# A hybrid SSD and attention layer on one Trainium2 core: ScalarE's own silu, modulation products in other places, and output weights split later

## The chip, the core and the metric

The kernel runs on one core of a Trainium2 chip. The core has a matrix engine (TensorE, PE in the profile; PEld is its weight load) and three engines for elementwise work: VectorE (DVE), ScalarE (ACT) and GpSimd (POOL). SyncE (SP) issues DMA transfers. Each engine takes its instructions in a fixed order, and waits on semaphores for the others. Matmuls write PSUM, and VectorE and ScalarE carry results from there into SBUF. The metric is the time of one execution on the device in microseconds (us), lower is better; the median of three runs is given.

## The reference, cut to what matters

One layer over 1024 tokens with D = 1024: a mixer with an SSD branch and an attention branch, then a convolutional feed-forward network (FFN). The vector c makes shifts, scales and gates (the modulations).

```python
mod = (silu(c) @ w_ada + b_ada)                       # 6 x 1024
sh_m, sc_m, g_m, sh_f, sc_f, g_f = split(mod, 6)
h = rmsnorm(x, norm_mix_w) * (1 + sc_m) + sh_m
z, xbc, dt_raw, q, k, v = split(h @ w_in, IN_SPLITS)  # 512, 1024, 8, 512, 512, 512
xbc = silu(causal_dwconv(xbc, conv_w) + conv_b)       # width 4; split into xs, B, C
dt = softplus(dt_raw + dt_bias);  A = -exp(a_log)
y = ssd_scan(xs * dt, dt * A, B, C) + d_skip * xs
y_ssd = rmsnorm(y * silu(z), ssd_norm_w)
y_att = chunk_attention(q, k, v, rel_bias)            # own chunk and 8 before it
x = x + g_m * (concat[y_ssd, y_att] @ w_out)
h = rmsnorm(x, norm_ffn_w) * (1 + sc_f) + sh_f
g, val = split(causal_dwconv(h @ w_up, ffn_conv_w), 2)
x = x + g_f * ((silu(g) * val) @ w_down)
return rmsnorm(x, final_norm_w)
```

All is float32.

## The kernel before

Each float32 matmul is made of three in a rounded format: both operands are split into a high part (a rounded copy, on ScalarE) and a low part (source minus high, on VectorE or GpSimd), and high x high, high x low and low x high are added in PSUM (`mm3`, L75 to L78; `split`, L80 to L86). The helper `split` with a scale does the rounding as a scaled copy (L82) and the low part as one VectorE operation (L83).

The span of 1223 us runs through these stages.

- To about 97 us: the modulations that the first norm needs, h transposed, and q, k, v. A modulation column is one VectorE product with a running sum, 128x1024, over 512 KB of w_ada that a DMA brings (`mod_col`, L134).
- To 319.5 us: attention, chunk by chunk. Its scheduling leaves VectorE places for modulation products; the last number of `MODS` says how many the end of attention takes.
- To about 375 us: the eight 128-channel tiles of xbc, `conv_silu`: B and C of each group (bt, ct), then the four of xs (xst). Per tile there are 48 matmuls into two banks (`s`), a scaled copy by ScalarE, three shifted VectorE products with a sum (L519), and silu as tanh (L524, ScalarE) and a product (L525, VectorE); the weights were halved ahead for that. Behind each tile's last such product `conv_mods` issues the number of modulation products that `CMODS` names, through three SBUF areas called wos. The weights of six of these tiles get their low part on GpSimd (L86, wl). The xs tiles are transposed by TensorE (tp, L597).
- To 424.9 us: z and dt_raw, as two halves of 260 columns (`z_tile`), half 1 first, eight row tiles of 24 matmuls each per half. A tile leaves PSUM by a tanh (L655, zt) and a VectorE product (L656, zs). Meanwhile the output weights w_out come in by DMA in eight slots (`wout_get`), go through three wos areas and two raws areas (`stage`), four of them are multiplied by the gate (`wout_fold`) and all are split (`wout_split`: slots 0 to 3 as 128x1024, slots 4 to 7 in two halves with the SSD norm's weight as a scale). `dt_prep` works out dt and the decays.
- To 531 us: the SSD in eight chunks. For each, `ssd_pre` makes the decay matrices of two groups (rm, sg, then an exponential L738 and a product L739), one chunk ahead; `ssd_y` does the state and output matmuls (ydp, yop, stp), adds, multiplies by silu(z) (L835) and normalises (L837 on ScalarE, two small GpSimd operations L116 and L117, L839 on ScalarE); `ssd_turn` transposes. Between them stand halves of the output projection (`wout_half`, tiles wops): half n takes the attention part (n even) or the SSD part (n odd) of a row tile. Each right side for it is split one half ahead (`wout_rhs`, yhl).
- To about 600 us: the second norm, h transposed, and the sums of a Strassen scheme for the FFN; the first products P1 of two units (uX) overlap with it. The rest is the FFN's units, to about 1000 us, and the down projection.

The order on each engine is fixed when the program is built: a scheduler takes the instructions in about the order in which the code is written, by their dependences and priorities, and `issue_after` or a pin forces one instruction behind another. `wout_split` is issued behind the last `ssd_pre` by two such pins (`pin`). Buffers are pools with a number of rotating tiles; a tile is free once its last reader is done. From `T.on = True`, and later `V.on = A.on = True`, TensorE, VectorE and ScalarE take the code's own order (`InOrder`; those rows have the line L58).

The loop over the chunks reads:

```python
for c in range(NT):
    y = ssd_y(c, *pre)
    if turn: ssd_turn(*turn)
    turn = (c, y)
    if c < NT - 1:
        pre = ssd_pre(c + 1, x_tile, sg_tile, lambda: wout_half(c, slice(0, 3)))
        row_scale(pin[0])
        wout_half(c, slice(3, 8))
```

Of the kernel before, what the change touches and what calls it, by code (L numbers as in the profile page):

```python
# [27 lines left out]
MODS = (0, 1, 1, 12)  # L28
CMODS = (1, 2, 2, 2, 2, 3, 3, 3)
# [35 lines left out]
def tile_block(ctx: ExitStack, tc: tile.TileContext, x, crep, pk, w_ada, w_first, w_ft, w_z,  # L65
# [145 lines left out]
    V.tensor_scalar(pkt[:, SCW:FCW], pkt[:, SCW:FCW], 0.5, None, op0=ALU.mult)  # L211
# [300 lines left out]
    def conv_silu(ft, dst, th2):  # L512
        wh, wl = early.pop(ft) if ft in early else wu_pair(w_ft[ft], A, G)
        ps = s_tile()
        gemm_ft(wh, wl, [ps[:, 0:512], ps[:, 512:1024]])
        w = [pkt[:, SCW + 4 * ft + j:SCW + 4 * ft + j + 1] for j in range(4)]
        A.activation(dst, ps, AF.Identity, scale=w[3], bias=pkt[:, SCB + ft:SCB + ft + 1])
        for j in range(1, 4):
            V.scalar_tensor_tensor(dst[:, j:S], ps[:, 0:S - j], w[3 - j], dst[:, j:S],  # L519
                                   op0=ALU.mult, op1=ALU.add)  # L520
        for hh in range(2):
            c = slice(hh * 512, hh * 512 + 512)
            th = th2()
            A.activation(th, dst[:, c], AF.Tanh)  # L524
            last = V.scalar_tensor_tensor(dst[:, c], th, 1.0, dst[:, c], op0=ALU.add, op1=ALU.mult)  # L525
        return last.ins
# [37 lines left out]
    na = bcp.tile([P, 16], F32, name="na")[:, 0:8]  # L564
# [15 lines left out]
    for g in range(2):  # L580
        conv_mods(2 * g, conv_silu(4 + g, bt_[g], th512))
        conv_mods(2 * g + 1, conv_silu(6 + g, ct_[g], th512))
# [8 lines left out]
    for ft in range(4):  # L591
        xt = bcp.tile([P, S], F32, tag="rm", bufs=2, name="xst")
        conv_mods(4 + ft, conv_silu(ft, xt, th512))
        for hh in range(2):
            tps = tp_tile()
            for j in range(4):
                T.transpose(tps[:, j * P:(j + 1) * P], xt[:, (4 * hh + j) * P:(4 * hh + j + 1) * P],  # L597
                            ident)
            A.activation(xs[:, 4 * hh:4 * hh + 4, ft * P:(ft + 1) * P],
                         tps.rearrange("p (a b) -> p a b", a=4), AF.Copy)  # L600
# [4 lines left out]
    def wout_load(dh, j):  # L605
        t = stage()
# [26 lines left out]
    def wz_weights(ch):  # L633
        ws = []
        for a in range(4):
# [4 lines left out]
            split(th_, tl_, t.rearrange("p (a b) -> p a b", a=2), A, V, scale=0.5)  # L640
            ws.append((th_, tl_))
        return ws

    def z_tile(ch, st, wz):
# [4 lines left out]
        for kt in range(KT):  # L649
# [3 lines left out]
        nz = 260  # L653
        th = wzp.tile([P, 272], F32, tag="zt", bufs=1, name="zt")
        A.activation(th[:, 0:nz], ps[:, 0:nz], AF.Tanh)  # L655
        V.scalar_tensor_tensor(zs[:, st, ch * 260:ch * 260 + nz], th[:, 0:nz], 1.0, ps[:, 0:nz],  # L656
                               op0=ALU.add, op1=ALU.mult)
        if ch == 1:
            V.scalar_tensor_tensor(zs[:, st, 512:520], ps[:, 252:260], 2.0,
                                   pkt[:, DTB:DTB + 8], op0=ALU.mult, op1=ALU.add)  # L660

    def dt_prep():
# [4 lines left out]
        A.activation(na, pkt[:, ALOG:ALOG + 8], AF.Exp)  # L667
# [83 lines left out]
    def wout_get(*slots):  # L751
        for j in slots:
            wt[j] = wout_load(*WORDER[j])
# [51 lines left out]
    def ssd_y(c, xdt, xdd, cb, ms_):  # L805
# [29 lines left out]
        V.tensor_tensor(y, y, zs[:, c, 0:512], ALU.mult)  # L835
# [4 lines left out]
        return y  # L840
# [27 lines left out]
    def wout_rhs(st, part):  # L868
        if st < NT:
            y = yq[st, part] = wu.tile([P, 2, 4, P], F32R, tag="wh", name="yhl")  # L870
            split(y[:, 0], y[:, 1], x1[part][:, st, :].rearrange("p (a b) -> p a b", a=4), A, V)

    def wout_half(n, ks=slice(0, 8), fill=()):
        st, part = n // 2, n % 2
        if ks.start == 0:
# [7 lines left out]
            for q in ((0,), (1, 2))[n] if n < 2 else (n + 1,):  # L883
                wout_rhs(q // 2, q % 2)
# [654 lines left out]
```

## Time and profile before

| what | value |
|---|---|
| median of 3 runs | 1224.7 us (1224.22 to 1227.89) |
| profiled execution: its own time | 1224.97 us |
| its span in the trace | 1223.3 us, 15651 instructions |
| mean granted TensorE clock | 0.99 |
| HBM read, written | 116.56 MB, 29.10 MB |

The busy share of TensorE in 40 slices of 30.6 us each, and the granted clock, in tenths:

| row | slices |
|---|---|
| PE | 5998899989999879999999999999999999999995 |
| PEclk | 9999999999999979999999999999999999999998 |

A digit 9 is 90% or more. The slices with a lower digit lie in the first 100 us, in attention, and around slice 14 (about 398 to 459 us), where the clock has its one 7. A row "PE x <- DVE y: 6.5, 1, 6.5" says that TensorE stood idle for 6.5 us in total, once, ahead of the instruction that writes x, until VectorE's y was done. A row with a time, as in "437.39 0.62 ACT L837 ACTIVATE yt<-yy", has the start in the span, the duration, the engine, the code line, the operation and output<-input.

### The profile page before, as it was taken

What the parts mean: (1) busy time and instruction counts of PE and PEld (TensorE: products, weight loads), DVE (VectorE), ACT (ScalarE), POOL (GpSimd) and SP (SyncE); (2) the same over time, 40 slices, a digit from 0 to 9 for tenths busy, and PEclk for the clock granted to TensorE, in tenths of its full rate; (3) what the DMA queues carried; (4) which work ended last, traced back from release to release, by engine and by line L of the source; (5) the groups of instructions that cost most, each with busy time, mean ns of one, the idle gap of its engine ahead of it and who ended that gap; (6) DMA issues with size and microseconds to landing.
All of it is one profiled execution on the core that took longest, in us unless ns stands there. A gap on an engine that the chain in (4) does not pass through costs nothing.

```text
span 1223.3 us, 15651 instructions
## 1 busy us (share of the span) xinstructions
PE 1161.6 (95%) x5802; PEld 975.8 (80%) x5802; DVE 943.2 (77%) x1421; ACT 588.3 (48%) x991; POOL 195.5 (16%) x172
## 2 busy tenths in 40 slices
PE   5998899989999879999999999999999999999995
PEld 3877787778779868888778888888888888888884
DVE  7846454698698758747999888988889869766976
ACT  4636454663343646666654433444434445433443
POOL 1205563773120124300000000000000000000002
PEclk9999999999999979999999999999999999999998
DMA  9722211314444301132123233232232277733533
GB/s 340 249 56 68 65 50 46 122 67 151 158 168 175 104 1 52 44 121 95 69 78 123 89 116 129 82 108 95 103 129 90 89 283 278 273 115 123 171 120 137
DMA packets 56395, 150.86 MB, mean 123 GB/s; under 512 B 5632, under 2 KB 5760, under 8 KB 54912
## 3 DMA queue, kind: packets, MB, share of 16 engines
q1 hardware_dynamic: 49264, 125.49, 30.3%
q10 hardware_dynamic: 7056, 24.38, 5.0%
q8 instruction: 45, 0.74, 0.3%
q14 instruction: 30, 0.25, 0.1%
HBM read 116.56 MB, written 29.10 MB: 119 GB/s over the span
## 4 chain that ended last, share of the span: by engine, by line
PE 81%; DVE 10%; ACT 3%; DMA 2%; issue 2%; POOL 1%; SPq 0%; DVEq 0%; POOLq 0%; ACTq 0%
PE wops L698 6%; PE dn L76 6%; PE dn L77 6%; PE dn L78 6%; PE uY L78 5%; PE uY L76 5%; PE uY L77 5%; PE uZ L76 3%; PE uZ L77 3%; PE uZ L78 3%; PE uX L76 3%; PE uX L78 3%; PE uX L77 3%; PE acc L76 2%; PE s L76 2%
## 5 line engine op out<-in xcount | busy, mean ns | idle before, releaser
L930 POOL TENSOR_TENSOR st<-st,mhalf 128x1 f32<-128x1 f32 x16 | 12.7, 798 | 689.4 <-DVE st L929 677.7
L76 PE MATMUL dn<-w 128*128 128x512 f32 x308 | 111.9, 389 | 0.0
L77 PE MATMUL dn<-w 128*128 128x512 f32 x308 | 111.9, 389 | 0.0
L418 POOL TENSOR_SCALAR p<-p,st 128x640 f32<-128x640 f32 (+4 forms) x64 | 99.5, 1570 | 42.7 <-DVE st L417 35.7
L78 PE MATMUL dn<-w 128*128 128x512 f32 x308 | 103.3, 389 | 0.0
L76 PE MATMUL uY<-tH,w 128*128 128x512 f32 x248 | 96.5, 389 | 0.0
L77 PE MATMUL uY<-tL,w 128*128 128x512 f32 x248 | 96.5, 389 | 0.0
L78 PE MATMUL uY<-tH,w 128*128 128x512 f32 x248 | 96.5, 389 | 0.0
L85 ACT ACTIVATE w<-ya 128x1024 fp32r<-128x1024 f32 (+1 forms) x41 | 39.1, 955 | 86.0 <-PE uY L78 79.4
L698 PE MATMUL wops<-hH,yhl 128*128 128x512 f32 x224 | 74.8, 402 | 3.5 <-DVE yhl L86 2.1
L77 PEld LDWEIGHTS dn<-w 128*128 128x128 f32 x308 | 57.8, 188 | 12.1
L78 PEld LDWEIGHTS dn<-w 128*128 128x128 f32 x308 | 57.8, 188 | 12.0
L76 PEld LDWEIGHTS dn<-w 128*128 128x128 f32 x308 | 57.8, 188 | 11.9
L85 ACT ACTIVATE w<-xs 128x1024 fp32r<-128x1024 f32 (+1 forms) x41 | 39.1, 954 | 35.6 <-PE uY L78 35.0
L76 PEld LDWEIGHTS uY<-tH,w 128*128 128x128 f32 x248 | 46.5, 188 | 9.7
L78 PEld LDWEIGHTS uY<-tH,w 128*128 128x128 f32 x248 | 46.5, 188 | 9.7
L77 PEld LDWEIGHTS uY<-tL,w 128*128 128x128 f32 x248 | 46.6, 188 | 9.6
L412 DVE CUSTOM_DVE_ANT_0 p<-s,bias 128x640 f32<-128x640 f32 (+4 forms) x64 | 40.4, 651 | 16.8 <-PE tp L444 5.2
L698 PEld LDWEIGHTS wops<-hH,yhl 128*128 128x128 f32 x224 | 42.3, 190 | 12.9 <-DVE yhl L86 2.5
L76 PE MATMUL s<-hH,wh 128*128 128x512 f32 x128 | 50.5, 394 | 1.4 <-DVE ct L519 1.2
L1089 DVE SCALAR_TENSOR_TENSOR a<-cv,pkt,a 128x1023 f32<-128x1023 f32 (+1 forms) x40 | 51.0, 1277 | 0.1
L415 ACT ACTIVATE p<-p,st 128x640 f32<-128x640 f32 (+4 forms) x64 | 44.1, 692 | 13.6 <-DVE st L412 13.3
(449 smaller groups left out, 3414.7 us busy)
## 6 DMA issues: line engine op xcount, KB each, us to landing
gz<-a ACTq DMA_DIRECT2D x10, 1024.0 KB, 5.3
wos<-in_w_ada_dram SPq DMA_DIRECT2D x18, 512.0 KB, 4.1
ya<-in_w_up_dram SPq DMA_DIRECT2D x11, 768.0 KB, 4.0
xs<-in_w_up_dram SPq DMA_DIRECT2D x11, 768.0 KB, 4.1
adat<-in_w_ada_dram SPq DMA_DIRECT2D x16, 512.0 KB, 5.1
raws<-in_w_ft_dram SPq DMA_DIRECT2D x14, 512.0 KB, 4.1
qk<-in_w_ada_dram SPq DMA_DIRECT2D x14, 512.0 KB, 4.6
gy<-a ACTq DMA_DIRECT2D x10, 512.0 KB, 2.6
```

What stands on the lines that cost most here:

```text
L76: T.matmul(ps, lh, rh, start=start, stop=False, skip_group_check=more)
L77: T.matmul(ps, lh, rl, start=False, stop=False, skip_group_check=more)
L78: T.matmul(ps, ll, rh, start=False, stop=stop, skip_group_check=more)
L85: i = A.activation(hi, src, AF.Copy) if ehi is A else ehi.tensor_copy(hi, src)
L412: V.tensor_tensor_reduce(out=dst, in0=src, in1=bsl, scale=-1.0, scalar=3e38, op0=ALU.add, op1=ALU.min, accum_out=nm)
L415: A.activation(pv_, pv_, AF.Exp, scale=-1.0, bias=nm, accum_out=rs)
L418: G.tensor_scalar(pv_, pv_, rr, None, op0=ALU.mult)
L698: i = op(*a, **k)
L930: G.tensor_tensor(r, ms, mhalf[:, 0:1], ALU.pow)
L1089: V.scalar_tensor_tensor(a[:, j:S], c[:, 0:S - j], w[2 - j], a[:, j:S], op0=ALU.mult, op1=ALU.add)
```

## The change

The change has eight parts.

1. `conv_silu` applies ScalarE's silu in place, and its VectorE product goes; the weights are not halved ahead. The low parts of six weight tiles are made on VectorE rather than on GpSimd.
2. Half 1 of z uses ScalarE's silu, and a VectorE addition of eight columns takes the place of two VectorE products. Half 0 is as before.
3. The exponential of a_log is issued at the start of the program. The table of ScalarE's functions is now loaded four times rather than twice.
4. Seven modulation products move from the end of attention into the convolutions.
5. The output weights are staged in other areas: slots 0 and 1 in tiles of the pool wu, slots 4, 5 and 2 in wos, 3 and 6 in raws, and 7 in wos again; they are loaded and folded at other times.
6. `dt_prep` and chunk 0's `ssd_pre` stand behind the first tile of z's half 0, ahead of the splits. Splits 4 to 7 are issued in the loop's first step, behind z's last tile.
7. The gate product and the norm of a chunk are a function of their own, `ssd_norm`. For chunks 0 and 1 it stands behind the preparation of the next chunk; for chunk 1 its product is issued behind the low part of the first SSD-side yhl. That split and the next attention-side one are written at other places.
8. Behind the last output half, the P1 product of the first unit gets its post-processing at once, and the preparation lo0 of a later product stands behind both units' P1.

The order of ScalarE at the end of z's half 0 and in the first chunk, before (hH are high parts of output weights, from the wos and raws areas; zt is z's tanh, rm and th belong to the decay matrices, yhl are right sides of the output projection):

```order
L82 ACTIVATE hH_84<-wos,pkt 128x512 x2
L82 ACTIVATE hH_84<-raws,pkt 128x512 x2
L82 ACTIVATE hH_84<-wos,pkt 128x512
L713 ACTIVATE rm<-tle_2878,adh 128x128 x4
L719 ACTIVATE rm<-tle_2878,adl 128x128 x3
L655 ACTIVATE zt<-s 128x260
L82 ACTIVATE hH_84<-wos,pkt 128x512
L82 ACTIVATE hH_84<-raws,pkt 128x512
L719 ACTIVATE rm<-tle_2878,adl 128x128
L82 ACTIVATE hH_84<-raws,pkt 128x512
L655 ACTIVATE zt<-s 128x260
```

and after:

```order
L85 ACTIVATE yhl<-ya 128x512
L660 ACTIVATE zt<-zps 128x260
L660 ACTIVATE zt<-s 128x260 x2
L82 ACTIVATE hH_84<-wos,pkt 128x512 x4
L82 ACTIVATE hH_84<-raws,pkt 128x512 x2
L82 ACTIVATE hH_84<-wos,pkt 128x512 x2
L828 ACTIVATE state_4055<-stp 128x512
L739 ACTIVATE th<-sg 128x512
L714 ACTIVATE rm<-tle_2865,adh 128x128 x4
L839 ACTIVATE yt,st_72<-yy 128x512
L841 ACTIVATE yy<-yy,st_72 128x512
L739 ACTIVATE th<-sg 128x512
```

The zt rows now stand ahead of all the L82 copies, and chunk 0's square and scale (L839, L841; L837 and L839 before) stand ahead of the second exponential of chunk 1.

VectorE at the same place, before (hL are low parts of output weights, zs the product that ends a tile of z):

```order
L86 TENSOR_TENSOR hL_85<-wos,hH_83 128x1024
L83 SCALAR_TENSOR_TENSOR hL_86<-wos,pkt,hH_84 128x512 x2
L83 SCALAR_TENSOR_TENSOR hL_86<-raws,pkt,hH_84 128x512 x2
L83 SCALAR_TENSOR_TENSOR hL_86<-wos,pkt,hH_84 128x512
L656 SCALAR_TENSOR_TENSOR zs<-zt,s 128x260
L83 SCALAR_TENSOR_TENSOR hL_86<-wos,pkt,hH_84 128x512
L83 SCALAR_TENSOR_TENSOR hL_86<-raws,pkt,hH_84 128x512 x2
L656 SCALAR_TENSOR_TENSOR zs<-zt,s 128x260
L831 TENSOR_TENSOR yy<-ydp,yy 128x512
L706 TENSOR_TENSOR xdt<-xs,sm_dt 128x512
L835 TENSOR_TENSOR yy<-yy,zs 128x512
```

and after:

```order
L661 SCALAR_TENSOR_TENSOR zs<-zt,zps 128x260
L661 SCALAR_TENSOR_TENSOR zs<-zt,s 128x260 x2
L83 SCALAR_TENSOR_TENSOR hL_86<-wos,pkt,hH_84 128x512 x4
L83 SCALAR_TENSOR_TENSOR hL_86<-raws,pkt,hH_84 128x512 x2
L829 TENSOR_TENSOR yy<-ydp,yy 128x512
L707 TENSOR_TENSOR xdt<-xs,sm_dt 128x512
L83 SCALAR_TENSOR_TENSOR hL_86<-wos,pkt,hH_84 128x512 x2
L837 TENSOR_TENSOR yy<-yy,zs 128x512
```

The two last zs now stand ahead of the eight L83, of which six stand ahead of the sum of ydp and two ahead of the gate product (L837).

ScalarE at the first products of the FFN, before (w are high parts of FFN weights, rb columns of h, cv the copy of a product of unit 0 or 1):

```order
L58 ACTIVATE ya<-xr,st_72 128x512
L58 ACTIVATE w<-ya 128x1024
L58 ACTIVATE rb_4975<-xps,bffn,affn 128x128 x4
L58 ACTIVATE cv<-uX 128x512 x2
L58 ACTIVATE t1h<-a 128x4x128
L58 ACTIVATE w<-xs 128x1024
```

and after:

```order
L58 ACTIVATE ya<-xr,st_72 128x512
L58 ACTIVATE cv<-uX 128x512
L58 ACTIVATE rb_4928<-xps,bffn,affn 128x128 x4
L58 ACTIVATE cv<-uX 128x512
L58 ACTIVATE w<-ya 128x1024
L58 ACTIVATE t1h<-a 128x4x128
L58 ACTIVATE w<-xs 128x1024
```

The first cv stands ahead of rb, and w behind the second cv.

The diff, cut to its core:

```diff
 EPS = 1e-6
...
-MODS = (0, 1, 1, 12)
-CMODS = (1, 2, 2, 2, 2, 3, 3, 3)
+MODS = (0, 1, 1, 5)
+CMODS = (2, 3, 3, 3, 3, 3, 4, 4)
...
-    V.tensor_scalar(pkt[:, SCW:FCW], pkt[:, SCW:FCW], 0.5, None, op0=ALU.mult)
+    na = const.tile([P, 16], F32, name="na")[:, 0:8]
+    A.activation(na, pkt[:, ALOG:ALOG + 8], AF.Exp)
...
-    def conv_silu(ft, dst, th2):
-        wh, wl = early.pop(ft) if ft in early else wu_pair(w_ft[ft], A, G)
+    def conv_silu(ft, dst):
+        wh, wl = early.pop(ft) if ft in early else wu_pair(w_ft[ft], A, V)
...
         for hh in range(2):
             c = slice(hh * 512, hh * 512 + 512)
-            th = th2()
-            A.activation(th, dst[:, c], AF.Tanh)
-            last = V.scalar_tensor_tensor(dst[:, c], th, 1.0, dst[:, c], op0=ALU.add, op1=ALU.mult)
+            A.activation(dst[:, c], dst[:, c], AF.Silu)
         return last.ins
 
...
-    wosc, stc_, pin = [0], [0], []
-
-    def stage():
-        i, stc_[0] = (0, 1, 2, 3, 4, 0, 1, 4)[stc_[0]], stc_[0] + 1
-        return wos[:, i, :] if i < 3 else raws[:, i - 3, :]
+    wosc, pin = [0], []
+
+    def stage(slot):
+        if slot < 2:
+            return wu.tile([P, D], F32, tag="wh", name="wst")
+        return raws[:, slot // 6, :] if slot in (3, 6) else wos[:, {4: 0, 5: 1}.get(slot, 2), :]
 
...
-            split(th_, tl_, t.rearrange("p (a b) -> p a b", a=2), A, V, scale=0.5)
+            split(th_, tl_, t.rearrange("p (a b) -> p a b", a=2), A, V, scale=(0.5, None)[ch])
...
+        if ch == 1:
+            A.activation(zs[:, st, 260:512], ps[:, 0:252], AF.Silu)
+            V.tensor_tensor(zs[:, st, 512:520], ps[:, 252:260], pkt[:, DTB:DTB + 8], ALU.add)
+            return
         th = wzp.tile([P, 272], F32, tag="zt", bufs=1, name="zt")
-        A.activation(th[:, 0:nz], ps[:, 0:nz], AF.Tanh)
-        V.scalar_tensor_tensor(zs[:, st, ch * 260:ch * 260 + nz], th[:, 0:nz], 1.0, ps[:, 0:nz],
-                               op0=ALU.add, op1=ALU.mult)
-        if ch == 1:
-            V.scalar_tensor_tensor(zs[:, st, 512:520], ps[:, 252:260], 2.0,
-                                   pkt[:, DTB:DTB + 8], op0=ALU.mult, op1=ALU.add)
+        zlast[:] = [A.activation(th[:, 0:nz], ps[:, 0:nz], AF.Tanh).ins,
+                    V.scalar_tensor_tensor(zs[:, st, ch * 260:ch * 260 + nz], th[:, 0:nz], 1.0, ps[:, 0:nz],
+                                           op0=ALU.add, op1=ALU.mult).ins]
 
...
     for st in range(NT):
         z_tile(1, st, wz)
         if st == 0:
...
-            wout_get(0, 1, 4)
+            wout_get(0, 1, 4, 5, 2)
...
-        if st in (3, 4, 5):
-            j = (0, 1, 4)[st - 3]
-            wout_fold(wt[j])
+        if st in (3, 4, 5, 6):
+            wout_fold(wt[(0, 1, 4, 5)[st - 3]])
     wz = wz_weights(0)
-    wout_get(5, 2)
+    wout_get(3, 6)
     for st in range(NT):
         z_tile(0, st, wz)
         if st == 0:
-            wout_fold(wt[5])
             dt_prep()
+            pre0 = ssd_pre(0, tp_tile, tp_tile)
+            pin0 = list(pin)
         if st == 3:
             for j in (0, 1, 2):
                 wout_split(j, wt[j])
-            wout_get(3, 6, 7)
-            pre0 = ssd_pre(0, tp_tile, tp_tile)
+            wout_get(7)
             wout_split(3, wt[3])
-        if st >= 4:
-            wout_split(st, wt[st])
...
+        return y, t
+
+    def ssd_norm(c, y, t, at=None):
+        with tc.issue_after(at) if at else ExitStack():
+            V.tensor_tensor(y, y, zs[:, c, 0:512], ALU.mult)
         ms = stat()
         A.activation(t, y, AF.Square, accum_out=ms)
         r = rstd(ms, 512.0 * EPS)
         A.activation(y, y, AF.Copy, scale=r)
-        return y
 
...
-            for q in ((0,), (1, 2))[n] if n < 2 else (n + 1,):
+            for q in ((0,), (2,))[n] if n < 2 else (n + 1,):
                 wout_rhs(q // 2, q % 2)
...
     pre, turn = pre0, None
     chain[:] = [None]
+    at = None
     for c in range(NT):
-        y = ssd_y(c, *pre)
+        y, t = ssd_y(c, *pre)
         if turn:
             ssd_turn(*turn)
+        if c == 1:
+            at = wout_rhs(0, 1)
+        if c > 1:
+            ssd_norm(c, y, t)
         turn = (c, y)
         if c < NT - 1:
             pre = ssd_pre(c + 1, x_tile, sg_tile, lambda: wout_half(c, slice(0, 3)))
+            if c < 2:
+                ssd_norm(c, y, t, at)
             row_scale(pin[0])
             wout_half(c, slice(3, 8))
+            if c == 0:
+                for j in range(4, 8):
+                    pin[:] = zlast
+                    wout_split(j, wt[j])
         else:
             wout_half(c)
     ssd_turn(*turn)
...
     wout_half(15, fill=([row(u0, 4), row(u0, 5)], [row(u1, 4)]))
+    u1.sums((5,))
+    u0.product("P1")
+    u1.product("P1", False)
+    h_raw((7,))
+    u1.post("P1")
     lo0 = u0.prep("Q5", "Q6", True)
-    u1.sums((5,))
-    for u in units:
-        u.product("P1", False)
-    h_raw((7,))
-    for u in units:
-        u.post("P1")
```

More of the change, by code (lines that the diff above doesn't have):

```diff
@@ L518, in conv_silu @@
         for j in range(1, 4):
-            V.scalar_tensor_tensor(dst[:, j:S], ps[:, 0:S - j], w[3 - j], dst[:, j:S],
-                                   op0=ALU.mult, op1=ALU.add)
+            last = V.scalar_tensor_tensor(dst[:, j:S], ps[:, 0:S - j], w[3 - j], dst[:, j:S],
+                                          op0=ALU.mult, op1=ALU.add)
         for hh in range(2):
             c = slice(hh * 512, hh * 512 + 512)
-            th = th2()
-            A.activation(th, dst[:, c], AF.Tanh)
-            last = V.scalar_tensor_tensor(dst[:, c], th, 1.0, dst[:, c], op0=ALU.add, op1=ALU.mult)
+            A.activation(dst[:, c], dst[:, c], AF.Silu)
         return last.ins
@@ L563, in tile_block @@
     sgtr = bcp.tile([P, P], F32R, name="sgtr")
-    na = bcp.tile([P, 16], F32, name="na")[:, 0:8]
     wos = bcp.tile([P, 3, D], F32, name="wos")
@@ L580, in tile_block @@
     for g in range(2):
-        conv_mods(2 * g, conv_silu(4 + g, bt_[g], th512))
-        conv_mods(2 * g + 1, conv_silu(6 + g, ct_[g], th512))
+        conv_mods(2 * g, conv_silu(4 + g, bt_[g]))
+        conv_mods(2 * g + 1, conv_silu(6 + g, ct_[g]))
     sgt_ = th512()[:, 0:P]
@@ L592, in tile_block @@
         xt = bcp.tile([P, S], F32, tag="rm", bufs=2, name="xst")
-        conv_mods(4 + ft, conv_silu(ft, xt, th512))
+        conv_mods(4 + ft, conv_silu(ft, xt))
         for hh in range(2):
@@ L603, in tile_block, with wout_load @@
     ws = [[], []]
-    def wout_load(dh, j):
-        t = stage()
+    def wout_load(slot):
+        (dh, j), t = WORDER[slot], stage(slot)
         for b in range(2):
@@ L666, in dt_prep @@
         A.activation(sm["e"], sm["nx"], AF.Exp)
-        A.activation(na, pkt[:, ALOG:ALOG + 8], AF.Exp)
         V.tensor_scalar(sm["t"], sm["e"], 2.0, None, op0=ALU.add)
@@ L752, in wout_get @@
         for j in slots:
-            wt[j] = wout_load(*WORDER[j])
+            wt[j] = wout_load(j)
     for st in range(NT):
@@ L870, in wout_rhs @@
             y = yq[st, part] = wu.tile([P, 2, 4, P], F32R, tag="wh", name="yhl")
-            split(y[:, 0], y[:, 1], x1[part][:, st, :].rearrange("p (a b) -> p a b", a=4), A, V)
+            return split(y[:, 0], y[:, 1], x1[part][:, st, :].rearrange("p (a b) -> p a b", a=4), A, V)[1].ins
     def wout_half(n, ks=slice(0, 8), fill=()):
```

2 lines of the change are left out of this document (1 added, 1 removed).

## The prediction

> **What bounds the kernel now.** I read the page first, for what is busy; then TensorE's waits; then windows around the waits; then the chain and the timeline inside those windows.
>
> ```profile
> PE 1161.6 (95%) x5802; PEld 975.8 (80%) x5802; DVE 943.2 (77%) x1421; ACT 588.3 (48%) x991; POOL 195.5 (16%) x172
> ```
>
> TensorE (PE) is busy for 95% of the span and the change takes no matmul from it. So the most that can be won is what TensorE loses to waits and to a throttled clock where the change works. The rows of its waits that lie there:
>
> ```profile
> PE ydp L698 <- DVE zs L656: 6.5, 1, 6.5
> PE wops L698 <- DVE yhl L86: 2.1, 1, 2.1
> PE uX L58 <- ACT cv L58: 1.7, 1, 1.7
> PE wops L698 <- ACT yhl L85: 1.4, 1, 1.4
> PE s L76 <- DVE ct L519: 1.2, 1, 1.2
> PE tp L597 <- DVE xst L525: 1.0, 1, 1.0
> ```
>
> The columns are the total, the number of waits and the longest, in us. The largest stands between the last matmul of z and the first of the SSD (ydp). The windows give each stretch as length, busy time of the engines (with counts), TensorE's granted clock, and the DMA share: the convolutions (two rows), the end of z, the gap, the output of chunks 0, 1 and 2, and the first Strassen products.
>
> ```profile
> core 0: us, PE busy (x) PEld busy (x) DVE busy (x) ACT busy (x) POOL busy (x), PEclk, DMA share, GB/s
> 320.00:345.00 25.00, 23.79 (x105) 19.38 (x105) 21.21 (x26) 5.47 (x6) 6.48 (x3) 1.00 0.71 239
> 345.00:370.00 25.00, 24.00 (x114) 19.62 (x113) 21.91 (x28) 10.96 (x18) 3.19 (x1) 1.00 0.48 162
> ...
> 424.90:431.37 6.47, 0.00 (x1) 0.00 (x1) 6.41 (x9) 5.39 (x15) 2.55 (x2) 0.69 0.00 0
> 431.37:444.32 12.95, 12.95 (x56) 11.33 (x57) 4.77 (x7) 6.37 (x18) 3.70 (x4) 0.76 0.00 0
> 444.32:461.02 16.70, 13.16 (x65) 10.71 (x64) 9.94 (x13) 8.30 (x23) 5.25 (x5) 0.90 0.05 17
> 461.02:472.03 11.01, 11.01 (x65) 9.62 (x64) 10.55 (x14) 5.70 (x14) 5.82 (x6) 1.00 0.06 24
> ```
>
> The 6.47 us gap costs more than itself: the clock is 0.69 in it, 0.76 in chunk 0's 12.95 us and 0.90 in chunk 1. Chunk 0 at full clock would take 12.95 x 0.76 = 9.8 us, so 3.1 us are lost to the clock there; in chunk 1 about 16.70 x 0.10 = 1.7 us, and 3.5 us to its two waits. The chain that ended last names what holds the gap and chunk 1:
>
> ```profile
> 423.77 4.21 DVE hL L83 x4
> ...
> 429.21 0.37 issue
> 429.58 1.40 DVE hL L83 x2
> 430.98 0.34 DVE zs L656
> ...
> 450.96 1.45 DVE yy L835
> ...
> 453.01 0.61 DVE yhl L86
> ```
>
> z's last two evacuations (zs) stand in VectorE's queue (DVE) behind the low parts of the output weights (hL), which nothing needs before chunk 1. In chunk 1 the low part of the attention half (yhl) stands behind the gate product (yy L835).
>
> **The change, part by part.** The sum is made against the profiled execution, 1224.97 us, of which the span is 1223.3; it lies 0.3 above the median of the three runs.
>
> *Convolutions and the first half of z.* These rows price what moves:
>
> ```profile
> L134 DVE CUSTOM_DVE_ANT_0 wos<-wos,rows x18: 1216/1221/3414, 323.3 to 383.6; 128x1024 f32<-128x1024 f32 x18
> L525 DVE SCALAR_TENSOR_TENSOR xst<-th,xst x8: 684/686/693, 347.2 to 380.7; 128x512 f32<-128x512 f32 x8
> wos<-in_w_ada_dram SPq DMA_DIRECT2D x18, 512.0 KB, 4.1
> 323.26 1.23 DVE L134 CUSTOM_DVE_ANT_0 wos<-wos,rows 128x1024 f32<-128x1024 f32 x1 [2.93 <-DMA wos<-in_w_ada_dram]
> 324.18 2.55 POOL L86 TENSOR_TENSOR wl<-raws,wh 128x1024 fp32r<-128x1024 f32 x1 [10.50 <-ACT wh L85]
> 324.41 3.41 DVE L134 CUSTOM_DVE_ANT_0 wos<-wos,rows 128x1024 f32<-128x1024 f32 x1
> ...
> 396.72 0.39 ACT L655 ACTIVATE zt<-s 128x260 f32<-128x260 f32 x1 [1.79 <-PE s L78]
> 397.14 0.42 DVE L656 SCALAR_TENSOR_TENSOR zs<-zt,s 128x260 f32<-128x260 f32 x1 [3.10 <-ACT zt L655]
> ```
>
> VectorE loses 16 products L525 (16 x 0.69 = 11.0 us) and 8 x 0.42 = 3.4 us of z. It gains 7 modulation products, 7 x 1.22 = 8.5 us, and 6 weight subtractions that POOL did in 2.55 us; on VectorE I estimate each at the 1.22 of a product of the same 128x1024 size: 7.3 us. That is +1.4 us, against 3.8 + 3.1 us of VectorE idle in the two windows. POOL's leaving helps: a product that met one took 3.41 instead of 1.22. ScalarE does a silu in place where it did a tanh, and is busy for only 5.47 and 10.96 us of the 25, so I cost that at nothing; its cover is the convolution matmuls. The seven products wait for nothing of TensorE but read 512 KB each, at a DMA share of 0.71 and 0.48: room, if not much. The 1.0 us wait of the transposes (xst L525) goes, since they now stand 25 matmuls later in TensorE's order. The 1.2 us wait (ct L519) stays: one product more and a subtraction now stand ahead of that row's work, and two products L525 and a stall of 2.2 us (3.41 - 1.22) no longer do. Together -1.0 us; bounds -2.2 (both waits gone) and +3 (a wait as long as two more products and a subtraction, 3 x 1.22, less the wait that is lost).
>
> *Table loads.* The exponential at the start brings ScalarE's first table load forward; two more switches come, one ahead of the first silu and one ahead of dt_prep's exponential.
>
> ```profile
> 4.59 1.28 ACT L192 ACT_TABLE_LOAD   x1 [4.59 <-DMA rows<-in_crep_dram]
> 295.75 1.16 ACT L524 ACTIVATE th<-bt 128x512 f32<-128x512 f32 x2 [4.19 <-DVE bt L519]
> ```
>
> ScalarE idled for 4.19 us ahead of the first of these places, which hides 1.28; were that cover gone, TensorE would wait up to 1.28 there. dt_prep loses two small operations and runs 20 matmuls ahead of its users. For the start I take +0.2 (bounds 0 and 1.28). The Trainium skill (ScalarE: Activation LUTs, What ACT_TABLE_LOAD costs) puts a switch at about 2.66 us with its drain; by that, too, the first would lie in the 4.19 us; the row's load alone is 1.28.
>
> *The gap at the end of z.* Splits 4 to 7 of the output weights (8 ScalarE and 8 VectorE operations) go behind z's last tile, and chunk 0's other preparation goes ahead of splits 0 to 3. Behind the last matmul then stand at most two tiles' tanh and product, 2 x (0.39 + 0.42) = 1.6, and some 0.4 for the hand-offs (0.37 for the longer one in the chain): 2.0 instead of 6.5, so -4.5. Bounds: 0, if something else holds VectorE as long; -5.5 with one tile behind.
>
> *Chunk 0.* If the gap is 2 us the clock should not fall, which is worth the 3.1. But the splits now run inside chunk 0, and its rows show who waits:
>
> ```profile
> 436.36 0.69 DVE L835 TENSOR_TENSOR yy<-yy,zs 128x512 f32<-128x512 f32 x1
> 437.39 0.62 ACT L837 ACTIVATE yt<-yy 128x512 f32<-128x512 f32 x1
> 439.46 0.66 POOL L116 TENSOR_SCALAR st<-st 128x1 f32<-128x1 f32 x1
> 440.21 0.57 POOL L117 TENSOR_TENSOR st<-st,mhalf 128x1 f32<-128x1 f32 x1
> 440.81 0.72 ACT L839 ACTIVATE yy<-yy,st 128x512 f32<-128x512 f32 x1 [1.06 <-POOL st L117]
> 441.44 0.58 ACT L738 ACTIVATE th<-sg 128x512 f32<-128x512 f32 x1
> 442.05 0.69 DVE L739 TENSOR_TENSOR th<-th,cb 128x512 f32<-128x512 f32 x1 [2.02 <-ACT th L738]
> ```
>
> ScalarE's exponential for the second group of chunk 1 (L738) stands behind chunk 0's normalisation (L839), and VectorE's product L739 behind that; ydp of chunk 1 reads it. After the last product of z, VectorE now has six splits (6 x 0.70 = 4.2, by 1.40 for two), the sum of ydp and the product for X (0.7 each, as the gate product of the same size), two more splits (1.4) and the gate product (0.7): 7.7 us. Then L837 0.6, POOL 1.3, L839 0.7, L738 0.6 and L739 0.7: 11.6 us, up to 13 if POOL's hand-offs (its 0.66 and 0.57 have 0.1 between and 1.5 ahead) come on top. TensorE needs 9.8 for its own work. I take 11.6 for the stretch, -1.35; bounds 9.8 (nothing waits, -3.1) and 16 (the clock falls too: 13 + 3, so +3). 11.6 is nearer to the sum of single durations, since no wait of before shows such a row.
>
> *Chunk 1.* The split yhl goes ahead of the gate product (1.45 less on its chain) and behind the previous product L739 (0.69): -0.8. Bounds -5.7 (it becomes chunk 2's 11.01) and +0.5 (the norm comes later).
>
> *First products of the FFN.* Rows of ScalarE where TensorE waited 1.7 us for cv:
>
> ```profile
> 581.74 1.06 ACT L58 ACTIVATE w<-ya 128x1024 fp32r<-128x1024 f32 x1
> 582.71 1.49 ACT L58 ACTIVATE rb<-xps,bffn,affn 128x128 f32<-128x128 f32 x4
> 584.08 1.09 ACT L58 ACTIVATE cv<-uX 128x512 f32<-128x512 f32 x2
> ```
>
> Now the first cv stands ahead of w and of the four rb, 2.55 us earlier. The wait goes: -1.6 (bounds -2 and 0, if the later w is waited for).
>
> Sum: -1.0 + 0.2 - 4.5 - 1.35 - 0.8 - 1.6 = -9.05; 1224.97 - 9.05 = 1215.9, so 1216.
>
> **The rivals.** *Nothing waits in chunks 0 and 1:* chunk 0 in 9.8 and chunk 1 in 11.5 make it -3.1 and -5.2 instead of -1.35 and -0.8: 1209.8. For it: chunk 2 has the same loop and takes 11.01 at clock 1.00. Against it: VectorE has 7.7 us of queue there that chunk 2 has not. A rule of the Trainium skill bears on the clock part of it (TensorE: Matmul & The Clock Gate, HAM oscillation): only idle gaps above some 3.4 us throttle. The trace agrees for the 6.47 us gap, and not for chunk 1, where 1.4 and 2.1 us of waiting brought 0.90; by the rule chunk 0's clock would be full.
>
> *The gap is filled again:* in the window of the gap VectorE is busy for 6.41 of 6.47 us; if the splits 0 to 3, now with more of chunk 0's preparation ahead of them, still queue before z's last product, the gap keeps some 4 us and the clock falls as before. Then -4.5 becomes -2.5 and the 1.35 and 0.8 vanish: 1224.97 - 1.0 + 0.2 - 2.5 - 1.6 = 1220.1; with a gap as long as before, 1222.6. Against it: the four splits are 4 x 1.22 us on VectorE, and end three tiles earlier.
>
> *Slower: the convolutions become bound by VectorE.* VectorE is at 21.2 and 21.9 of 25 us; each product is issued behind a convolution's last accumulation and waits for its 512 KB. If the products hold VectorE at their DMA's pace, the next accumulation comes late and its matmuls find no free buffer. One such product at 3.41 costs 2.2. The rest of the sum is -8.05, so it decides beyond 8 + 3.7 = 11.8 us of loss, more than five such products; at seven, 15.4 us: 1224.97 - 8.05 + 15.4 = 1232.3. For it: VectorE once waits 2.93 us for this DMA; against it, POOL's operations, beside which the 3.41 stood, have left this stage.
>
> **How the numbers follow.** Forecast 0.57 (its own range 1212 to 1219), nothing waits 0.17, gap filled 0.16, slower 0.10. A difference under 0.3% (3.7 us) is about what a measurement of this kernel cannot tell from none; faster is then the first two and a little of the third, 0.76; same the rest of it, 0.14; slower 0.10. The range 1208.5 to 1222.5 takes in the first two and nearly all of the third, and leaves out the slower case and the extremes.
>
> **What would show it.** Right: the wait of ydp for zs is under 2.5 us, no clock below 0.95 between the end of z and chunk 1, the row of cv at uX is gone, and xst no longer delays the transposes. Chunk 1's ydp waits for th L739 (L740 after the change) by 1 to 3 us. Wrong: a row of TensorE waits above 3 us in the convolutions, for ct or xst or for a weight's low part; a clock still near 0.76 in chunk 0; or a new wait for w at the first FFN products.

## The result

The changed kernel takes 1224.1 us (median of 20 runs), the kernel before 1226.1 us (20 runs): ratio 0.9984, with a 95% interval of 0.9975 to 0.9993. It is faster, but by 2 us and not by the 9 that were forecast, and it lies above the range.

The profiled execution after takes 1222.88 us with a span of 1221.2, against 1224.97 and 1223.3. TensorE's waits, after, where the change works:

```profile
PE s L76 <- ACT xst L518: 2.0, 1, 2.0
PE ydp L699 <- DVE zs L661: 1.6, 1, 1.6
PE wops L699 <- DVE yhl L86: 1.5, 1, 1.5
PE wops L699 <- ACT yhl L85: 1.4, 1, 1.4
...
PE ydp L699 <- DVE th L740: 0.3, 1, 0.3
```

The wait of the first ydp fell from 6.5 to 1.6 us; those for cv and of the transposes for xst are gone. The windows of the gap and of chunks 0, 1 and 2, after:

```profile
core 0: us, PE busy (x) PEld busy (x) DVE busy (x) ACT busy (x) POOL busy (x), PEclk, DMA share, GB/s
425.31:427.21 1.90, 0.28 (x4) 0.07 (x2) 0.85 (x2) 1.29 (x4) 1.66 (x2) 1.00 0.00 0
427.21:438.70 11.49, 11.49 (x54) 9.86 (x55) 10.78 (x14) 7.88 (x18) 4.04 (x5) 0.85 0.00 1
438.70:453.78 15.08, 11.80 (x63) 9.65 (x62) 9.94 (x14) 10.20 (x30) 4.76 (x5) 1.00 0.00 1
453.78:464.83 11.05, 11.05 (x63) 9.62 (x62) 10.44 (x14) 6.46 (x17) 5.73 (x6) 1.00 0.13 47
```

So the work did get shorter here. The starts of marked matmuls in both traces tell where the gain stands and where it ends (a plain table of start times in us, worked out from the two traces):

| first matmul of | before | after | after - before |
|---|---|---|---|
| last pv of attention | 319.19 | 320.44 | +1.25 |
| last of z | 424.61 | 425.31 | +0.70 |
| ydp, chunk 0 | 431.37 | 427.21 | -4.16 |
| ydp, chunk 1 | 444.16 | 438.70 | -5.46 |
| ydp, chunk 2 | 460.86 | 453.78 | -7.08 |
| uX | 576.53 | 569.36 | -7.17 |
| uZ | 590.31 | 581.42 | -8.89 |
| dn | 999.88 | 995.60 | -4.28 |
| end of the last matmul | 1209.48 | 1207.41 | -2.07 |

Here uX, uY and uZ are the products of the FFN's units, and dn is the down projection. At the first uZ the changed kernel is 8.9 us ahead. Then, over 626 us in which it shows one wait, of 0.4 us (the kernel before has one there too, of 1.2), it gives back 6.8. The same 550 us of the FFN and the down projection, before and after:

```profile
640.00:1190.00 550.00, 550.00 (x2428) 455.44 (x2427) 463.23 (x541) 234.47 (x266) 0.00 (x0) 1.00 0.40 140
```

```profile
640.00:1190.00 550.00, 550.00 (x2399) 449.67 (x2398) 457.82 (x533) 233.97 (x265) 1.19 (x2) 1.00 0.39 139
```

TensorE is busy throughout at the full granted clock, and yet does 2399 matmuls where it did 2428. The pitch, the mean time from the start of one matmul to the start of the next, is 550 us over the count: 229.3 ns instead of 226.5. The code of this stage is the same. The groups by line show it, first before and then after (the columns behind the bar are busy us, and the mean ns of one; that is above the pitch, since one matmul starts before the last has ended):

```profile
L76 PE MATMUL dn<-w 128*128 128x512 f32 x308 | 111.9, 389 | 0.0
L76 PE MATMUL uY<-tH,w 128*128 128x512 f32 x248 | 96.5, 389 | 0.0
```

```profile
L76 PE MATMUL dn<-w 128*128 128x512 f32 x308 | 112.6, 391 | 0.0
L76 PE MATMUL uY<-tH,w 128*128 128x512 f32 x248 | 97.2, 392 | 0.0
```

What differs in this stage is where the tiles lie. The exponential of a_log moved to the start, and its tile na, 64 bytes a partition, into the pool of constants. The pools are placed from two sides of SBUF, left (low addresses) and right. The compiled programs place all later pools of the left side behind that one: three of the FFN's five weight tiles w start at byte 3456, 11648 and 19840 before and 64 bytes later after, and so do tH and tL (36224 and on). The other two weight tiles and the b11, b21 and t1 tiles lie on the right side and keep their places.

### The profile page after: what moved, and what is told of

The parts are those of the page before. It is cut to its first block, busy times and chain, and to the rows that moved or that the text cites. A ratio compares the mean times of both kernels' runs of the same rounds, so it can differ in the third digit from the quotient of the medians.

```text
span 1221.2 us, 15631 instructions
## 1 busy us (share of the span) xinstructions
PE 1167.3 (96%) x5802; PEld 974.5 (80%) x5802; DVE 928.8 (76%) x1402; ACT 592.0 (48%) x993; POOL 174.3 (14%) x166
## 4 chain that ended last, share of the span: by engine, by line
PE 82%; DVE 9%; ACT 3%; issue 2%; DMA 2%; POOL 1%; SPq 0%; DVEq 0%; POOLq 0%; ACTq 0%
PE dn L76 6%; PE dn L77 6%; PE dn L78 6%; PE wops L699 5%; PE uY L76 4%; PE uY L78 4%; PE uY L77 4%; PE uX L78 3%; PE uX L76 3%; PE uZ L77 3%; PE uZ L76 3%; PE uX L77 3%; PE uZ L78 3%; PE s L76 3%; PE s L77 3%; PE s L78 3%
## 5 line engine op out<-in xcount | busy, mean ns | idle before, releaser
L77 PEld LDWEIGHTS uY<-tL,w 128*128 128x128 f32 x248 | 46.6, 188 | 10.2
L413 DVE CUSTOM_DVE_ANT_0 p<-s,bias 128x640 f32<-128x640 f32 (+4 forms) x64 | 40.4, 651 | 17.5 <-PE tp L445 5.2
L86 DVE TENSOR_TENSOR pt<-tp,pt 128x512 fp32r<-128x512 f32 (+2 forms) x72 | 41.5, 595 | 13.1 <-ACT pt L85 12.8
```

Of the source, the lines that this page charges most:

```text
L77: T.matmul(ps, lh, rl, start=False, stop=False, skip_group_check=more)
L86: return i, elo.tensor_tensor(lo, src, f32(hi), ALU.subtract)
L413: V.tensor_tensor_reduce(out=dst, in0=src, in1=bsl, scale=-1.0, scalar=3e38, op0=ALU.add, op1=ALU.min, accum_out=nm)
```

## The experiments

### Is it the place of the tiles?

A matmul has two operands: the stationary one, 128x128, which a PEld row loads, and the moving one, 128x512, which the MATMUL row reads. Theory A: the starts of a matmul's operands set its pitch. Theory B: moved work or transfers beside the FFN do. Four kernels test them. The first gave the changed kernel's na 128 bytes.

```diff
-    na = const.tile([P, 16], F32, name="na")[:, 0:8]
+    na = const.tile([P, 32], F32, name="na")[:, 0:8]
```

> The changed kernel, but the tile na that it adds to the pool of constants has 128 bytes a partition instead of 64, so that every tile allocated behind it starts at a multiple of 128 bytes again, as before the change. Instructions and their order are the same. Theory A (addresses): the 6.7 us that the changed kernel gives back from the first uY to the end are matmuls whose operands start 64 bytes off; the matmul pitch in the FFN returns from 229.4 to 226.7 ns and the time is 1224.1 - 6.7 = 1217.4 us, ratio to before 0.993. Theory B (order and traffic: the FFN's matmuls are slowed by other transfers or by work that now stands beside them): nothing changes, pitch 229.4 ns and 1224.1 us, ratio 0.998.

Measured: 1226.5 us, ratio 1.0003 (0.9992 to 1.0014). Neither theory had said that: it is slower than the changed kernel's 1224.1, and starts at multiples of 128 bytes are not what it takes. The other three are the kernel before with nothing but unused bytes; the second adds a tile to the constants.

```diff
     bffn = const.tile([P, 8], F32, name="bffn")
+    const.tile([P, 16], F32, name="pad64")
```

> The kernel before with one unused tile of 64 bytes a partition in the pool of constants, nothing else. Theory A (addresses): the FFN's pitch goes from 226.7 to 229.4 ns, the stretch from the first uY to the end grows by 6.7 us, 1232.8 us, ratio 1.0055; the stages ahead of it keep their times. Theory B (order and traffic): nothing changes, 1226.1 us, ratio 1.000.

Measured: 1233.4 us, ratio 1.0058 (1.0045 to 1.0071), where 1.0055 was expected. From the first uY to the end it takes 621.1 us instead of 613.7. 64 unused bytes cost 7 us.

The third adds them ahead of the pool of h, tH and tL alone, so that only moving operands shift; the fourth adds both, so that the weights shift by 64 and tH by 128.

```diff
     es_ht = ExitStack()
+    es_ht.enter_context(tc.tile_pool(name="padl", bufs=1, side="left")).tile([P, 16], F32, name="padl")
```

> The kernel before with 64 unused bytes ahead of the pool that holds h and the Strassen sums tH and tL: 1056 of the FFN's 2772 matmuls have a moving operand that starts at 64 modulo 128, all stationary operands start at 0. Theory A (addresses), with the 229.4 ns that this class has in the changed kernel's trace: 1056 x 2.7 ns = 2.9 us more, 1229 us, ratio 1.0024; if only the stationary side matters, 0. Theory B (order and traffic): ratio 1.000.

> The kernel before with 64 unused bytes in the pool of constants and 64 more ahead of the pool of h, tH and tL: the first three of the five weight tiles of the FFN's ring start 64 bytes off, tH and tL do not. 1308 of 2772 matmuls have an aligned moving operand and a stationary one at 64. Theory A (addresses), with the 233.2 ns of that class in the changed kernel's trace: 1308 x 6.5 ns = 8.5 us, and about 1 us for the others: 1235.5 us, ratio 1.0078. If only the moving side matters, under 2 us. Theory B (order and traffic): ratio 1.000.

Measured: ratio 1.0037 (1.0024 to 1.0050) and 1.0083 (1.0070 to 1.0096). That is 4.5 us where 2.9 were expected, and 10.2 where 9.5 were. Theory B is out: in these three no instruction differs from the kernel before.

Why then did 128 bytes not help? I sorted the matmuls of each trace in the same window of 550 us by the start of their moving operand and of the stationary operand that the next matmul loads beside them (the addresses are those of the compiled programs), and took the mean time from one start to the next:

| kernel | stationary start minus moving start, modulo 256 | matmuls | pitch, ns |
|---|---|---|---|
| before | 0 for all | 2426 | 226.7 |
| after | 0 | 1274 | 227.9 |
| after | 64 | 572 | 233.0 |
| after | 192 | 551 | 229.2 |
| na at 128 bytes | 0 | 1267 | 227.7 |
| na at 128 bytes | 128 | 1123 | 232.7 |
| moving side shifted | 0 | 1471 | 227.7 |
| moving side shifted | 192 | 936 | 229.8 |
| stationary side shifted | 0 | 729 | 228.1 |
| stationary side shifted | 64 | 561 | 232.8 |
| stationary side shifted | 128 | 385 | 233.2 |
| stationary side shifted | 192 | 714 | 229.0 |

It is the difference between the two that counts, not the start of either: after the change, 864 matmuls have both operands shifted by 64, and take 228.0. With na at 128 bytes the left side lies 128 away from the right. Whether it is the next matmul's stationary operand or the matmul's own is not shown: in each trace the two start at the same place modulo 256 for all but some 90 matmuls. Theory A2 follows: a matmul keeps the short pitch where its moving operand and the stationary one beside it start at the same place modulo some power of two. Its test moves na into unused columns of another constant, so that nothing shifts.

```diff
-    amix = const.tile([P, 16], F32, name="amix")[:, 0:8]
+    amna = const.tile([P, 16], F32, name="amix")
+    amix, na = amna[:, 0:8], amna[:, 8:16]
...
-    na = const.tile([P, 16], F32, name="na")[:, 0:8]
```

> The changed kernel, but na takes eight unused columns of the tile amix, so that the pool of constants does not grow and every tile of the left side starts where it did before the change (weights of the FFN at 3456, h and the sums at 36224). Theory A2 (relative addresses: a matmul runs at 226.7 ns where its moving operand and the stationary operand loaded beside it start at the same place modulo 512 bytes, and at 229 to 233 ns where they do not): FFN pitch 226.7 ns, and the changed kernel gains the 6.7 us, 1224.1 - 6.7 = 1217.4 us, ratio to before 0.993. Theory B2 (the padded run's failure to get faster means that the FFN of the changed kernel is slowed by something else): pitch above 229 ns, 1224 us, ratio 0.998.

Measured: 1217.4 us, ratio 0.9924 (0.9909 to 0.9940): what A2 said. That it agrees to a tenth of a microsecond is luck, since the six runs lie between 1213.9 and 1220.2. It beats both kernels, and its window of the FFN counts as before the change:

```profile
640.00:1190.00 550.00, 550.00 (x2428) 455.44 (x2427) 463.84 (x542) 236.36 (x270) 2.65 (x2) 1.00 0.40 140
```

Two more sizes of the unused tile in the kernel before give the period and the grain (the smallest difference that counts): `[P, 64]` (256 bytes) and `[P, 8]` (32 bytes).

> The kernel before with 256 unused bytes a partition in the pool of constants: left and right tiles then differ by 256 modulo 512 in their starts. Theory A2 with a period of 512 bytes: about as in the run with 128 bytes, pitch about 230 ns, 6 to 8 us more, ratio 1.005 to 1.007. With a period of 256 bytes: pitch 226.7 ns, ratio 1.000. Theory B2: ratio 1.000.

> The kernel before with 32 unused bytes a partition in the pool of constants: left and right tiles of the FFN differ by 32 modulo 256. Relative addresses modulo 256 at a grain of 32 bytes or finer: the FFN's pitch rises to about 229 to 230 ns, 6 to 8 us more, ratio 1.005 to 1.0065. At a grain of 64 bytes: 226.7 ns and ratio 1.000.

Measured: with 256 bytes ratio 0.9998 (0.9989 to 1.0007), with 32 bytes 1.0096 (1.0079 to 1.0112). Their windows, 256 first:

```profile
640.00:1190.00 550.00, 550.00 (x2428) 455.44 (x2427) 463.14 (x542) 234.36 (x266) 0.00 (x0) 1.00 0.40 139
```

```profile
640.00:1190.00 550.00, 550.00 (x2388) 447.86 (x2387) 454.60 (x529) 229.77 (x260) 0.00 (x0) 1.00 0.40 139
```

The period is 256 bytes, and 32 bytes already count; less was not tried. A shift of 32 costs more than one of 64, because both of its unequal classes, 32 and 224, are slow (233.3 and 233.4 ns), where of 64 and 192 only the first is; and it costs more than the 6 to 8 us that I had expected: about 12.

### Do the steps ahead of the FFN do what the prediction said?

The next four take the kernel with na in amix (1217.4 us), where no shift disturbs, and undo one part each. The first issues the splits 4 to 7 behind z's tiles 4 to 7 again.

```diff
             wout_split(3, wt[3])
+        if st >= 4:
+            wout_split(st, wt[st])
...
-            if c == 0:
-                for j in range(4, 8):
-                    pin[:] = zlast
-                    wout_split(j, wt[j])
```

> The run with na in amix, but the splits 4 to 7 of the output weights are issued behind z's tiles 4 to 7 as before, not behind z's last tile; the first chunk's preparation stays ahead. The order on VectorE puts the eight low parts ahead of the last two zs. If the place of these splits is what shortened the wait of the first ydp (1.9 us from the last z matmul in the changed kernel, 6.8 before): 5 to 6.8 us again, chunk 0 at a lower clock, 4 to 6 us slower than the run with na in amix, ratio to before 0.996 to 0.998. If it was the earlier preparation of chunk 0 alone: 2 us as in the changed kernel, and the ratio of the run with na in amix.

Measured: ratio 0.9973 (0.9963 to 0.9983), 5 to 6 us slower. The wait is back, longer than before, with VectorE busy in it, and the clock falls to 0.78 in it and 0.74 in chunk 0 (the row of waits, then the window from the last z matmul to the first ydp):

```profile
PE ydp L699 <- DVE zs L661: 7.7, 1, 7.7
```

```profile
424.16:432.09 7.93, 0.28 (x3) 0.07 (x1) 7.33 (x10) 4.92 (x10) 2.89 (x2) 0.78 0.00 0
```

So the place of these splits wins the gap, not the earlier preparation of chunk 0, which this kernel keeps. The clock in chunk 0 tells less: it is 0.74 in the profile with na in amix too, where the gap is 1.96 us.

The second puts the code at the first FFN products back (lo0 first, both products, then both posts).

```diff
+    lo0 = u0.prep("Q5", "Q6", True)
     u1.sums((5,))
-    u0.product("P1")
-    u1.product("P1", False)
+    for u in units:
+        u.product("P1", False)
     h_raw((7,))
-    u1.post("P1")
-    lo0 = u0.prep("Q5", "Q6", True)
+    for u in units:
+        u.post("P1")
```

> The run with na in amix, but the code at the first FFN products is in its old order (lo0 first, both P1 products, then both posts). If that order is what won 1.7 us between the first uX and the first uZ (13.78 before, 12.06 in the changed kernel): 13.8 again and 1.5 to 2 us slower than the run with na in amix. If that gain came from the earlier stages: 12.1 and the same time.

Measured: ratio 0.9938 (0.9925 to 0.9951), whose interval meets that of 0.9924; the trace tells more. From uX to uZ it takes 13.85 us, against 11.80 with na in amix, and the wait is there again:

```profile
PE uX L58 <- ACT cv L58: 1.8, 1, 1.8
```

The third gives the convolutions' low parts back to GpSimd.

```diff
-        wh, wl = early.pop(ft) if ft in early else wu_pair(w_ft[ft], A, V)
+        wh, wl = early.pop(ft) if ft in early else wu_pair(w_ft[ft], A, G)
```

> The run with na in amix, but the low parts of the six convolution weights are made on GpSimd as before. If VectorE's taking them is what keeps the convolutions from gaining more (it loses 11.0 us of L525 and gets 7.3 us of low parts): the stretch from the last pv to the last z matmul falls below the 104.6 us of that run. If it frees VectorE of the products that took 3.41 us beside a GpSimd operation: the stretch grows by 1 to 2 us, towards the 105.4 us of before or over it, and the waits for ct and for the transposes return.

Measured: ratio 0.9928 (0.9902 to 0.9953), not to be told from 0.9924. From the last pv to the last z matmul it took 106.6 us, in which the clock stood at half for 3.41 us, which costs 1.7; without that it is 104.9, against 104.6. The wait of s for ct is 2.6 us, against 2.1 at that place with na in amix, the wait of the transposes stays away, and one modulation product beside a GpSimd operation takes 3.42 us again. In the total, these runs show no difference between the two engines.

The fourth puts the gate product and the norm back; only VectorE's order in chunk 1 differs.

```diff
         y, t = ssd_y(c, *pre)
+        ssd_norm(c, y, t)
         if turn:
             ssd_turn(*turn)
-        if c == 1:
-            at = wout_rhs(0, 1)
-        if c > 1:
-            ssd_norm(c, y, t)
...
-            if c < 2:
-                ssd_norm(c, y, t, at)
...
-            for q in ((0,), (2,))[n] if n < 2 else (n + 1,):
+            for q in ((0,), (1, 2))[n] if n < 2 else (n + 1,):
```

> The run with na in amix, but with the gate product and the norm of each chunk where they were, and the right sides yhl split at their old places. The order changes on VectorE alone, in chunk 1: the gate product stands ahead of both low parts yhl again. By the prediction's term for chunk 1 (0.8) that stretch grows by 0.8 to 1.5 us, with the wait for yhl L86 near 2.1 instead of 1.5, and the waits of chunk 0 stay; if the order does not matter there, the 1.5 us wait stays as it is. A clock window of 3.41 us more or less, worth 1.7 us, may come on top.

Measured: ratio 0.9940 (0.9922 to 0.9958), not to be told from 0.9924. The wait for yhl L86 is 1.3 us, not 2.1, so the expected row did not come. Chunk 1 took 21.4 us, but with the clock at half for 13.7 of them, which hides waits; this run does not settle what the order in chunk 1 is worth. Its chunk 0 ran at full clock, in 11.01 us with the wait of ydp for th in view, 1.03 us there and 0.66 behind it.

## Why the prediction was wrong, point by point

**The step that failed** is the one on the exponential at the start. It priced the instruction and its table load (+0.2; attention's first s matmul comes 0.15 us later in the trace of after, and at the same time as before with na in amix) and gave nothing to the tile na, which the same lines move into the pool of constants. That term is missing from the sum. Its size is +6.7 us: 1224.1 against 1217.4 with na in amix (7.1 us if each is counted from the runs of before beside it). None of the rivals had it either: each put its loss into a wait or a busy engine, and the loss is in neither. The addresses stand in the compiled program and no view of the profile shows them, but the diff shows a new tile in a pool that others follow.

**The rest of the sum came out right in total, its terms only in part.** -9.05 us was forecast; the kernel with na in amix takes 9.1 us less than the 1226.5 of before in its runs. That -8.89 stood at the first uZ is one pair of executions: the six traces of the kernel before and its padded copies, which run the same instructions, reach uZ at 589.9 to 594.2 us, and the three of the changed kernel, with na at 64 bytes, at 128 and in amix, at 581.4, 586.8 and 583.7. The gap and the first FFN products are steady in these traces (6.76 to 6.80 against 1.90 to 1.98 us, and 13.75 to 13.98 against 11.80 to 12.06). Chunks 0 and 1 are not (12.4 to 13.6 against 11.5 to 13.1, and 16.7 to 17.5 against 15.1 to 17.4): with na in amix each had two steps at half clock, and took as long as before:

```profile
core 0: us, PE busy (x) PEld busy (x) DVE busy (x) ACT busy (x) POOL busy (x), PEclk, DMA share, GB/s
426.15:439.22 13.07, 13.07 (x55) 11.37 (x55) 11.41 (x15) 9.74 (x23) 3.98 (x5) 0.74 0.00 1
439.22:456.58 17.36, 14.43 (x63) 11.70 (x62) 9.29 (x13) 9.53 (x27) 4.75 (x5) 0.80 0.04 16
```

The terms, by the traces of before and after where no other is named:

- *The gap:* 2.0 us forecast, 1.90 measured; with the splits ahead, 7.93. Right, and for the reason given.
- *Chunk 0:* 11.6 forecast, 11.49 measured; that the two agree is luck. The prediction had the clock at full and ydp waiting for th by 1 to 3 us. In this execution TensorE is busy for all of the 11.49 us at a clock of 0.85, half for 3.41 us, which is 9.8 us of work and 1.7 lost to the clock; the wait for th is 0.3, behind the first eight matmuls of ydp. So the premise that the clock does not fall behind a gap of 2 us failed here. Where the clock stays at full, as in the kernel with low parts on GpSimd, the forecast's case is to be seen, only shorter, 11.06 us with 1.1 of waiting:

```profile
PE ydp L699 <- DVE th L740: 1.1, 1, 1.1
```

```profile
427.36:438.42 11.06, 9.97 (x55) 8.39 (x55) 10.83 (x15) 8.98 (x21) 4.24 (x5) 1.00 0.00 0
```

The chain that ended last, after, has the way it named: the splits, the gate product, the square, GpSimd's two operations, the scale, the exponential, th, and ydp.

```profile
432.66 2.11 DVE hL L83 x2
434.77 1.46 DVE yy L837
...
436.32 0.73 ACT yt L839 x2
...
437.45 0.58 POOL st L117
438.06 0.72 ACT yy L841
438.78 0.49 ACT th L739
439.30 0.70 DVE th L740
440.00 0.04 issue
440.04 1.12 PE ydp L699 x8
```

- *Chunk 1:* -0.8 forecast, -1.62 in these two traces (16.70 to 15.08). The wait for yhl fell by 0.6, the clock in it is 1.00 instead of 0.90, which is worth up to 1.7, and 0.3 of waiting for th came in. How much of it the new order brought, and whether the term holds at all, stays open, by the last run and the 17.36 us above.
- *First FFN products:* -1.6 forecast, -1.72 measured (13.78 to 12.06), and back with the old order. Right.
- *Convolutions and z:* -1.0 forecast, -0.55 measured (105.42 to 104.87 from the last pv to the last z matmul). That is within what traces of the same instructions scatter (104.9 to 105.5 before). The wait of the transposes went as said. The other one, 1.2 us for ct, is 2.0 at the same place: counted from the end of attention, the last accumulation of ct (L520) ends 0.8 us later (the profile names ScalarE's copy xst, which ends 0.1 us behind it). In VectorE's queue ahead of it stand two products that waited for their transfer (the group of products first, with the shortest, median and longest in ns, then the two):

```profile
L134 DVE CUSTOM_DVE_ANT_0 wos<-wos,rows x25: 1209/1219/1227, 324.3 to 386.2; 128x1024 f32<-128x1024 f32 x25
...
331.80 1.22 DVE L134 CUSTOM_DVE_ANT_0 wos<-wos,rows 128x1024 f32<-128x1024 f32 x1 [0.33 <-DMA wos<-in_w_ada_dram]
...
334.73 1.23 DVE L134 CUSTOM_DVE_ANT_0 wos<-wos,rows 128x1024 f32<-128x1024 f32 x1 [0.49 <-DMA wos<-in_w_ada_dram]
```

That is the rival of the slower convolutions in small, in this trace; in the three kernels above with the old splits, the old FFN order and the old norm, whose convolutions are the same, the wait is 1.3 to 1.6. None of the 25 products takes 3.41 us any more; the longest takes 1.23.

- *Table loads:* the one ahead of the first silu takes 1.28 us behind 4.11 of idle time, as was said:

```profile
289.38 1.28 ACT L524 ACT_TABLE_LOAD   x1 [4.11 <-DVE bt L520]
```

- *Attention,* which no term touched, ended 1.25 us later in this execution, with 3.41 us at half clock from 241.4 us on; the trace of before has no such window there. It is 1.7 us that a run has or has not.

**The base:** the three runs of before gave 1224.7; in 20 runs its median is 1226.1. From there, -9.05 leads to 1217.0, and the kernel with na in amix came to 1217.4.

Of the rivals, the filled gap gave 1220.1 to 1222.6, near the measured time, but for something that did not happen: the gap closed. That nothing waits in chunks 0 and 1 did not come either: chunk 1 waits for yhl and th, and chunk 0 waits for th where its clock is full.

## What to carry to other kernels

A new tile, however small, moves every tile allocated behind it in its pool's side: before a change is priced, compare the start addresses of the operands of the matmuls that fill the time, and if they move, pad or reuse spare columns until they agree again. What must agree here is the start of the moving and of the stationary operand modulo 256 bytes, over the whole ring of tiles. A pitch that changes in a stage whose code is the same, with TensorE 100% busy at full clock, is the sign; count matmuls in equal windows.

## What the runs showed of the hardware that I had not expected

- A 128x512 matmul in this kernel has a pitch of 226.7 ns, constant within 1 ns, where all moving and stationary operands start at the same place modulo 256 bytes. Where they differ, the means of a class are 233.3 ns (by 32), 232.8 to 233.0 (64), 232.6 to 233.2 (128), 228.8 to 229.8 (192) and 233.4 (224); equal pairs in a kernel that has both kinds take 227.7 to 228.3. The profile shows these matmuls as busy, and no wait. Why they take longer is not shown; that the two reads meet in memory would be a guess.
- By the trace's record of the clock it fell to half behind a wait of only 1.9 us, in steps of 3.41 us: for one step in the changed kernel's profile, two in that with na in amix, and for none behind the same gap with low parts on GpSimd, where one came later, at 440 us. Such a step costs up to 1.7 us, and the profiles of kernels with the same work here differ in where it stands. The Trainium skill (TensorE: Matmul & The Clock Gate, What's actually happening) gives a free-running window of 3413 ns, and the steps agree with it. The same page's rule (HAM oscillation) that idle gaps over some 3.4 us are what brings the clock down does not cover these: no gap there was longer than 2 us.
